# Moving GpSimd's drain from a critical section's exit to the end of its own gather stream

## The chip, the cores and the metric

One core of one Trainium2 chip. The metric is the device time of one execution in microseconds. Every time below is a median over repeated executions unless it is called a single run. "Span" is the length of the profiled execution, about 1.7 us shorter than the device time of the same execution.

## The reference

```python
B, S, N, D = (16, 4096, 2048, 512)
gathered = x[b_idx, indices, :].copy()      # x [B,S,D] f32, indices [B,N], sorted
cs = np.cumsum(gathered, axis=1)            # running sum along the gathered rows
return np.matmul(cs, w).astype(np.float32)  # w [D,D]
```

67 MB of rows are gathered and 67 MB of results stored.

## The kernel before

The kernel is written engine by engine, with its own semaphores, inside one critical section. GpSimd generates 256 gathers of 128 rows, ScalarE casts the gathered tiles and evicts results, TensorE does triangular sums and the projection, VectorE carries the running sum, and SyncE issues the stores. `pool.need(s, v)` makes GpSimd wait until semaphore `s` has reached `v`; `sp.need` does the same for SyncE. There are T = 256 gathers, R = 2 of them to a group, G = 128 groups, NG = 16 gather buffers and NO = 8 output buffers. The parts that matter here:

```python
ctx.enter_context(tc.tile_critical(no_gpsimd_drain=False))
# ... (cut)
def gather(t):
    g, r = divmod(t, R)
    pool.need(s_c, g + 1 - NG // R)          # a buffer is free again
    # ... (cut: which index column)
    nc.gpsimd.indirect_dma_start(
        out=g32[g % (NG // R)][:, r, :], out_offset=None, in_=x_flat,
        in_offset=bass.IndirectOffsetOnAxis(ap=ap, axis=0),
        element_offset=(t // NT) * S * D,
    ).then_inc(s_g[t % NG], 16)
# ... (cut) SyncE: all stores, then it waits until the last ones have landed
for g in range(G):
    store(g)
for g in range(G - NO, G):
    sp.need(s_o[g % NO], 16 * (g // NO + 1))
# ... (cut) GpSimd: two masks, then all gathers
for t in range(T):
    gather(t)
```

When the section ends, SyncE, which by then has waited for the last stores, raises a semaphore. Each of the five engines answers it with a drain, and SyncE waits for the five answers, for GpSimd's with its no-op. After that comes the program's closing barrier, in which GpSimd has three more drains of its own. None of this is in the source; it stands in the built program.

Of the kernel before, what the change touches and what calls it, by code (L numbers as in the profile page):

```python
# [27 lines left out]
def kernel(  # L28
# [7 lines left out]
    nc = tc.nc  # L36
# [38 lines left out]
    pa = [ps.tile([P, DC, R, Q], FP32, name=f"pa{i}") for i in range(NA)]  # L75
    pb = [ps.tile([P, R, D], FP32, name=f"pb{i}") for i in range(NB)]

    ctx.enter_context(tc.tile_critical(no_gpsimd_drain=False))  # L78

    def sem(name):  # L80
        return tc.alloc_semaphore(name)
# [17 lines left out]
    def gather(t):  # L99
        g, r = divmod(t, R)  # L100
        pool.need(s_c, g + 1 - NG // R)
        if t < FIRST:
            pool.need(s_first, 16)
            ap = idx_first[:, t, 0:1]
        else:
            pool.need(s_prep, t // P + 1)
            ap = idxg[:, t // P, t % P : t % P + 1]
        nc.gpsimd.indirect_dma_start(  # L108
            out=g32[g % (NG // R)][:, r, :],
            out_offset=None,  # L110
            in_=x_flat,
# [3 lines that stand above are left out]
# [103 lines left out]
    ).then_inc(s_ut, 1)  # L218
    for t in range(T):
        gather(t)  # L220


    for k in range(KI):
# [65 lines left out]
```

## Time and profile before

| | before |
|---|---|
| device time | 357.12 us median of 3 (356.56 to 357.59) |
| span of the profiled run | 354.6 us |
| bytes moved | 135.92 MB, about 415 GB/s in the body |
| GpSimd's drain at the exit | 348.56 to 353.53 us |

The instructions that matter are not counted as busy work: drains, no-ops and semaphore instructions stand in the views with a "q" behind the engine's name (POOLq is GpSimd's sequencer) and only when a source line is asked for. So the busy rows of the page show an empty end, and the queue's waits and the lines of the exit tell what fills it.

### The profile page before, as it was taken

How to read it: one execution, taken by the hardware profiler on the slowest of the kernel's cores; microseconds unless marked ns; L12 is line 12 of the kernel's file. 1: busy time of each engine (PE TensorE's matmuls, PEld its weight loads, DVE VectorE, ACT ScalarE, POOL GpSimd, SP SyncE). 2: the span in 40 equal slices, each digit the busy share in tenths (PEclk: the TensorE clock that was granted, in tenths of full speed). 3: DMA queues.
4: the chain of work that ended last, by engine and by line, in shares of the span. 5: the costliest groups of instructions: out<-in, count | busy, mean ns of one | idle time of the engine just before them, and what ended most of it. 6: DMA issues, size and time to landing. Idle time of an engine off the chain costs nothing.

```text
span 354.6 us, 5833 instructions
## 1 busy us (share of the span) xinstructions
PE 301.8 (85%) x2050; PEld 149.2 (42%) x2050; DVE 178.1 (50%) x260; ACT 257.9 (73%) x258; POOL 243.7 (69%) x264
## 2 busy tenths in 40 slices
PE   0497799999899999899898988989989889898880
PEld 0253354444354444444444444444444444444440
DVE  1354465555555555555554554645555555555530
ACT  0776687787788787777777777877878778687760
POOL 6777777777777777777777777777777777774000
PEclk9999999999999999999999999999999999999995
DMA  6789999999999999999999999999999999999761
GB/s 222 224 241 384 409 410 401 415 411 418 412 417 416 415 414 415 413 416 416 415 415 414 414 413 413 411 417 415 413 417 413 416 413 414 412 415 414 293 244 74
DMA packets 40029, 135.92 MB, mean 383 GB/s; under 512 B 6465, under 2 KB 6721, under 8 KB 40001
## 3 DMA queue, kind: packets, MB, share of 16 engines
q0 software_dynamic: 20480, 67.13, 48.5%
q1 hardware_dynamic: 19520, 68.43, 47.8%
q8 instruction: 17, 0.28, 0.3%
q14 instruction: 12, 0.09, 0.1%
HBM read 68.42 MB, written 67.11 MB: 382 GB/s over the span
## 4 chain that ended last, share of the span: by engine, by line
POOL 50%; DMA 22%; issue 17%; PE 5%; ACT 3%; ACTq 0%; SPq 0%
POOL g L108 50%; DMA g<-in_x_dram,idxg 21%; PE pb L160 4%; ACT g L120 3%; PE pa L128 1%; ACT ob L172 1%; DMA idx_first<-in_indices_dram 1%; ACTq L23 0%; SPq L284 0%; SPq L78 0%
## 5 line engine op out<-in xcount | busy, mean ns | idle before, releaser
L108 POOL DMA_INDIRECT g<-in_x_dram,idxg x254 | 240.5, 947 | 77.4 <-issue 71.3
L160 PE MATMUL pb<-w,cst 128*128 128x512 f16 x1024 | 263.5, 381 | 0.0
L148 DVE TENSOR_TENSOR cst<-pa,cst 128x512 f16<-128x512 f32 x240 | 166.0, 692 | 138.1 <-PE pa L128 137.3
L120 ACT CAST g<-g 128x1024 f16<-128x1024 f32 x128 | 133.6, 1045 | 66.9 <-issue 32.2
L172 ACT COPY ob<-pb 128x1024 f32<-128x1024 f32 x128 | 129.2, 1010 | 11.4 <-PE pb L160 9.8
L128 PE MATMUL pa<-ut,g 128*128 128x128 f16 x1024 | 101.1, 222 | 38.5 <-ACT g L120 37.8
L128 PEld LDWEIGHTS pa<-ut,g 128*128 128x128 f16 x1024 | 69.4, 99 | 128.4 <-ACT g L120 97.6
L160 PEld LDWEIGHTS pb<-w,cst 128*128 128x128 f16 x1024 | 90.0, 98 | 62.0 <-issue 1.1
L143 DVE CAST cst<-pa 128x512 f16<-128x512 f32 x16 | 11.1, 692 | 20.4 <-PE pa L128 20.4
L120 ACT ACT_TABLE_LOAD x1 | 1.3, 1283 | 9.5 <-DMA g<-in_x_dram,idx_first 9.5
L229 PE MATMUL pb<-ident,idxf 128*128 128x128 f32 x2 | 0.9, 462 | 4.2 <-DVE idxf L225 4.2
L108 POOL DMA_INDIRECT g<-in_x_dram,idx_first x2 | 2.1, 1043 | 1.6 <-DMA idx_first<-in_indices_dram 1.3
L225 DVE CAST idxf<-idx 128x128 f32<-128x128 uint32 x2 | 0.5, 226 | 4.1 <-DMA idx<-in_indices_dram 4.1
L229 PEld LDWEIGHTS pb<-ident,idxf 128*128 128x128 f32 x2 | 0.4, 182 | 4.4 <-issue 4.2
L252 ACT CAST w<-w 128x2048 f16<-128x2048 f32 x1 | 1.9, 1892 | 0.0
L234 DVE CAST idxg<-pb 128x128 uint32<-128x128 f32 x2 | 0.6, 292 | 0.3
L198 POOL MEMSET ident<- 128x128 f32 x1 | 0.2, 205 | 0.5 <-SPq L78 0.5
L201 POOL TENSOR_SCALAR_AFFINE_SELECT ident<-ident 128x128 f32<-128x128 f32 x1 | 0.3, 288 | 0.1
L273 POOL MEMSET const-float32-0.0<- 128x1 f32 x1 | 0.1, 100 | 0.3 <-issue 0.3
L210 POOL TENSOR_SCALAR_AFFINE_SELECT ut<-ut 128x128 f16<-128x128 f16 x1 | 0.3, 292 | 0.0
L199 POOL MEMSET ut<- 128x128 f16 x1 | 0.2, 206 | 0.0
L273 POOL MEMSET const-uint8-127<- 128x1 uint8 x1 | 0.1, 117 | 0.0
(2 smaller groups left out, 0.2 us busy)
## 6 DMA issues: line engine op xcount, KB each, us to landing
out_dram<-ob SPq DMA_DIRECT2D x128, 512.0 KB, 7.2
g<-in_x_dram,idxg POOLq DMA_INDIRECT x254, 10.2
w<-in_w_dram SPq DMA_DIRECT2D x1, 1024.0 KB, 5.6
idx<-in_indices_dram SPq DMA_DIRECT2D x2, 128.0 KB, 2.3
g<-in_x_dram,idx_first POOLq DMA_INDIRECT x2, 5.1
idx_first<-in_indices_dram SPq DMA_DIRECT2D x1, 2.0 KB, 1.9
```

The source lines that it names most:

```text
L108: nc.gpsimd.indirect_dma_start(out=g32[g % (NG // R)][:, r, :], out_offset=None, in_=x_flat, in_offset=bass.IndirectOffsetOnAxis(ap=ap, ax ...
L120: nc.scalar.copy(out=g16[g % NH][:], in_=g32[g % (NG // R)][:]).then_inc(s_c, 1)
L128: mm = nc.tensor.matmul(out=pa[t % NA][:, c], lhsT=g16[g % NH][:, r, c * P : (c + 1) * P], rhs=ut[:], start=(c == 0), stop=(c == DC - 1),)
L143: nc.vector.tensor_copy(out=dst, in_=pa[t % NA][:]).then_inc(s_d, 1)
L148: nc.vector.tensor_tensor(out=dst, in0=pa[t % NA][:], in1=last.unsqueeze(2).broadcast_to([P, DC, R, Q]), op=mybir.AluOpType.add,).then_inc ...
L160: mm = nc.tensor.matmul(out=pb[g % NB][:, j], lhsT=cst[g % NC][:, c, j, :], rhs=w16[:, c, :], start=(c == 0), stop=(c == DC - 1),)
L172: nc.scalar.copy(out=ob[g % NO][:], in_=pb[g % NB][:]).then_inc(s_e, 1)
L201: nc.gpsimd.affine_select(out=ident[:], in_=ident[:], compare_op=mybir.AluOpType.is_equal, fill=0.0, base=0, pattern=[[-1, P]], channel_mu ...
L225: nc.vector.tensor_copy(out=idxf[:, k, :], in_=idx64[:, k, 0::2]).then_inc(s_if, 1)
L229: nc.tensor.transpose(out=pb[k % NB][:, 0, :P], in_=idxf[:, k, :], identity=ident[:]).then_inc(s_pt, 1)
L234: nc.vector.tensor_copy(out=idxg[:, k, :], in_=pb[k % NB][:, 0, :P]).then_inc(s_prep, 1)
L252: nc.scalar.copy(out=w16[:], in_=w32[:]).then_inc(s_wc, 1)
```

## The change

The intent is to take GpSimd's drain off the end of the program: it drains in its own stream, behind its last gather, where it has nothing else to do, and the exit asks GpSimd for a no-op only.

```diff
-    ctx.enter_context(tc.tile_critical(no_gpsimd_drain=False))
+    ctx.enter_context(tc.tile_critical(no_gpsimd_drain=True))
 ...
     for t in range(T):
         gather(t)
+    nc.gpsimd.drain()
```

The closing barrier and its drains are the same in both.

## The prediction

> **What bounds the kernel now.** I read the page's slices first, because the change touches no arithmetic and I wanted to know where the span stops being limited by the steady state.
>
> ```profile
> POOL 6777777777777777777777777777777777774000
> ...
> DMA  6789999999999999999999999999999999999761
> GB/s 222 224 241 384 409 410 401 415 411 418 412 417 416 415 414 415 413 416 416 415 415 414 414 413 413 411 417 415 413 417 413 416 413 414 412 415 414 293 244 74
> ```
>
> From the fourth slice to the 37th the DMA engines are at nine tenths or more and move about 415 GB/s: the body is bound by bytes, 67 MB gathered and 67 MB stored. One slice is 354.6/40 = 8.87 us. In the last slice the traffic falls to 74 GB/s, so a slice at the end is nearly empty. GpSimd, which issues the gathers, is done about three slices before the end. The diff touches only GpSimd's stream after its last gather and the exit, so next comes the timeline of the end (start, duration, then engine and work; releaser in brackets).
>
> ```profile
> 322.66 0.95 POOL L108 DMA_INDIRECT g<-in_x_dram,idxg  x1 [0.30 <-issue]
> ...
> 344.63 1.01 ACT L172 COPY ob<-pb 128x1024 f32<-128x1024 f32 x1 [0.71 <-PE pb L160]
> 345.67 0.33 SPq L178 DMA_DIRECT2D out_dram<-ob  x1
> ```
>
> GpSimd's last gather is generated at 322.66 + 0.95 = 323.6 us. The last eviction ends at 345.64, the last store is issued at 345.67. After that no engine computes, yet the span ends at 354.6, which is 8.9 us later. Three stretches of that end (columns: length, busy time of PE, weight loads, DVE, ACT, GpSimd, granted clock, DMA share, GB/s):
>
> ```profile
> 345.60:348.50 2.90, 0.00 (x0) 0.00 (x0) 0.00 (x0) 0.04 (x1) 0.00 (x0) 0.71 0.60 242
> 348.50:353.60 5.10, 0.00 (x0) 0.00 (x0) 0.00 (x0) 0.00 (x0) 0.00 (x0) 0.50 0.00 0
> 353.60:354.60 1.00, 0.00 (x0) 0.00 (x0) 0.00 (x0) 0.00 (x0) 0.00 (x0) 0.50 0.00 0
> ```
>
> The first stretch is the last stores landing. In the second, 5.1 us long, nothing computes and nothing moves. What SyncE's queue waits for from 345 us on, and the instructions of the section's exit (line 78: count, duration in ns min/median/max, first and last start), say why:
>
> ```profile
> SPq L78 <- POOLq L78: 4.8, 1, 4.8
> SPq L23 <- DMA out_dram<-ob: 2.1, 2, 1.5
> ...
> L78 SPq NOP  x2: 13/16/18, 0.8 to 353.6; - x2
> ...
> L78 ACTq DRAIN  x1: 8/8/8, 348.6 to 348.6; - x1
> L78 POOLq DRAIN  x1: 4965/4965/4965, 348.6 to 348.6; - x1
> L78 DVEq DRAIN  x1: 17/17/17, 348.6 to 348.6; - x1
> ```
>
> At 348.6, once SyncE has seen the last stores land, every engine drains. Four of them take 7 to 17 ns; GpSimd takes 4965 ns, and SyncE's no-op at 353.6 waits for it: 4.8 us of wait, 1.3% of the time. The page's chain of work that ended last stops at ACT's copy at 344.63; the drain, not counted as busy, does not show in it. Behind the exit comes the program's own closing barrier (line 284), which also has drains on GpSimd:
>
> ```profile
> L284 POOLq DRAIN  x3: 34/34/123, 353.6 to 354.3; - x3
> ```
>
> These cost 34, 123 and 34 ns, directly behind the long one.
>
> **What the Trainium skill says.** "Perfetto Trace Analysis", section "Sequencer-only Instruction (DRAIN, etc)", says that for such an instruction the profiler's start is the moment all its semaphores are satisfied. So the 4965 ns are the drain itself and not its wait for SyncE; the trace agrees, as it starts at 348.6 together with the others'. "PSUM — Partial Sum Buffer", on sequencer-only instructions and completion, says that "drain waits for the engine to go fully idle", while a no-op is no sign of completion. "DMA: Bandwidth & Descriptors", section "SWDGE vs HWDGE vs iDMA", says that GpSimd's DMAs are descriptors that its own cores compute in software and append to rings in SBUF. Only GpSimd has such software here, and only its drain is long; that fits a drain which settles those rings, but no row shows what the drain does. VectorE's page, "VectorE: DVE Perf Modes", section "The DRAIN you can't avoid", gives runtime drains as about 12 ns on all five engines; the 4965 ns here disagree for GpSimd, and the measurement decides.
>
> **The change part by part.** 1. It adds one drain to GpSimd's stream, directly behind the 256th gather, at 323.6. 2. At the exit it replaces GpSimd's drain by a no-op which waits for the same semaphore from SyncE and answers on the same one; the other four engines' drains stay. The built instruction streams of PE, DVE, ACT and SyncE are otherwise equal. 3. The closing barrier keeps GpSimd's three drains, the first of which now follows the no-op.
>
> Part 1 costs nothing on the path if it is over by 348.5. Two sizes: the drain just takes 4965 ns, over at 328.6; or it also waits for the gathers in flight. The packets of GpSimd's queue end at 337.0, and then another 4965 ns gives 342.0. Both are ahead of 348.5, with 19.9 and 6.5 us to spare. GpSimd has nothing else to do then, and all gathers are already issued, so no transfer starts later.
>
> Part 2: before, the path is: SyncE's signal 348.52, drain 348.56 to 353.53, SyncE's no-op 353.55. After: signal 348.52, GpSimd's no-op at 348.56 for about 0.02 (SyncE's own is 13 to 18 ns). SyncE is then itself still collecting the other engines' answers: its last such instruction starts at 348.743 and takes 28 ns, so its no-op can run at about 348.80. The saving is 353.55 - 348.80 = 4.75 us, which agrees with the 4.8 of the wait view.
>
> Part 3: if the first closing drain stays at 34 ns, it adds nothing. Sum: 357.12 - 4.75 = 352.4 us, ratio 1.0135.
>
> **The rivals.** (a) The drain is deferred, not removed: the first drain after GpSimd has been standing idle for 25 us pays, whichever it is. Then the closing drain takes the 4.97 us and the time stays at 357.1. For it: all the cheap closing drains follow an expensive one immediately, so the trace never shows a late first drain cheap. Against it: the very first drain of the program takes 187 ns, part of that under a memset, with no gather yet issued; the long one is the only one with gathers between it and the one before. No packet moves between 348.5 and 353.6, so it isn't an instruction fetch that the trace would show. (b) The early drain settles only what has landed by 323.6. A gather takes 10.2 us at the median to land and 1.25 us to issue, so some 8 to 12 of 256 are then in flight. If the cost is per gather, 4965/256 = 19 ns each, the closing drain would pay about 0.2 us: 352.6. If it is a fixed cost for rings with anything in them, it would pay all of 4.97 again: 357.1. (c) The early drain disturbs the last transfers, by work on the rings while 10 gathers are in flight. The last casts wait for such gathers (the cast at 335.47), so a delay there would reach the end; a loss of up to 1 us is my guess at its size, 353.4. Nothing in the profile speaks for it.
>
> **Range and chances.** I give 0.77 to the full saving, landing at 351.6 to 353.0, since the three runs of before spread over 1.0 us; 0.08 to a part of it (rival b per gather, or c), 353 to 355.5; 0.15 to none of it, 356.5 to 357.7. A range of 351.4 to 355.5 then holds it somewhat over 8 times in 10. Faster by over 2% needs 350.0 or less, that is 7.1 us saved: more than the whole drain, and the rest of the tail is stores landing and the barrier, which stay. Slower by over 2% would need 7 us of new wait. So: faster 0.01, within 2% 0.98, slower 0.01.
>
> **What would show it right or wrong.** Right: a GpSimd drain starting at about 323.6, over before 348.5; no 5 us stretch without traffic after the last store; SyncE's wait for GpSimd at the exit under 0.2 us; closing drains still at tens of ns; a span of about 349.8. The early drain's length (5 or up to 18 us) tells whether it waits for the gathers in flight. Wrong: a closing drain on GpSimd of about 4.9 us, with the span still at 354.6 (rival a, or b with a fixed cost), or casts late at the end with landing times over the present ones (c).

## The result, and the profile after

| | before | after |
|---|---|---|
| device time, median of 6 | 356.99 us (356.45 to 357.88) | 352.50 us (351.85 to 353.14) |
| span of the profiled run | 354.6 us | 351.3 us |
| GpSimd at the exit | drain, 4965 ns | no-op, 13 ns |
| SyncE's exit signal to its no-op | 5.03 us | 0.29 us |

The ratio is 0.9872, 95% interval 0.9851 to 0.9893. A ratio here is the mean time of one kernel's fast runs over that of the other's in the same rounds, so not quite the ratio of the medians.

The slices of the profiled run after, to be held against those of before: GpSimd's row, DMA share and GB/s in 40 slices of 8.8 us.

```profile
POOL 6777777777777777777777777777777777776000
DMA  6789999999999999999999999999999999999854
GB/s 219 229 233 378 408 411 412 416 414 417 416 417 414 417 415 415 415 414 416 413 417 413 416 411 407 414 414 417 412 417 411 417 413 416 411 414 416 345 229 181
```

The body is the same, near 415 GB/s. Only the end is shorter: the last slice now averages 181 GB/s instead of 74. Three stretches of the end (length; busy time of PE, weight loads, DVE, ACT, GpSimd; granted clock; DMA share; GB/s):

```profile
345.80:350.00 4.20, 0.00 (x0) 0.00 (x0) 0.00 (x0) 0.00 (x0) 0.00 (x0) 0.80 0.42 170
350.00:350.40 0.40, 0.00 (x0) 0.00 (x0) 0.00 (x0) 0.00 (x0) 0.00 (x0) 0.50 0.00 0
350.40:351.30 0.90, 0.00 (x0) 0.00 (x0) 0.00 (x0) 0.00 (x0) 0.00 (x0) 0.50 0.00 0
```

The dead stretch of 5.1 us between the last store and the closing barrier has shrunk to 0.4. GpSimd's instructions by source line, after (count; duration in ns min/median/max; first and last start): the exit (78), the new drain (221) and the closing barrier (285).

```profile
L78 POOLq NOP  x1: 13/13/13, 350.0 to 350.0; - x1
...
L221 POOLq DRAIN  x1: 21874/21874/21874, 318.3 to 318.3; - x1
...
L285 POOLq DRAIN  x3: 34/41/123, 350.1 to 351.1; - x3
```

The new drain runs from 318.3 to 340.2, some 10 us ahead of the exit, and the closing drains stay at tens of ns.

One trap lies in comparing just these two profiles. Their spans differ by 3.3 us, not by 4.7. In the run after, SyncE, having seen its last store land, signals the exit at 349.99 instead of 348.52, 1.47 us later. Most of this, 1.3 us, is that this store took 3.6 us from its issue to its last packet where it took 2.3 in the run before. Adding the 1.47 back gives 3.27 + 1.47 = 4.74 us, which is the difference of the two exits, 5.03 - 0.29. The same store took 2.3 us in the profiles of experiments 1, 2 and 3 and 3.6 in that of experiment 4, so a profiled pair carries 1.3 us of chance here. Why it varies stayed open.

### The profile page after: what moved, and what is told of

Read it like the earlier page. It is cut to its first block, busy times and chain, and to the rows that moved or that the text cites. A ratio compares the mean times of both kernels' runs of the same rounds, so it can differ in the third digit from the quotient of the medians.

```text
span 351.3 us, 5834 instructions
## 1 busy us (share of the span) xinstructions
PE 301.2 (86%) x2050; PEld 149.0 (42%) x2050; DVE 178.2 (51%) x260; ACT 258.1 (73%) x258; POOL 243.7 (69%) x264
## 4 chain that ended last, share of the span: by engine, by line
POOL 48%; DMA 26%; issue 17%; PE 4%; ACT 3%; POOLq 0%; ACTq 0%; SPq 0%
POOL g L108 48%; DMA g<-in_x_dram,idxg 25%; PE pb L160 3%; ACT g L120 2%; PE pa L128 1%; DMA idx_first<-in_indices_dram 1%; POOLq L221 0%; ACT ob L172 0%; ACTq L23 0%; SPq L285 0%; SPq L78 0%
```

## The experiments

Three theories could explain the result. A: gathers leave work behind for GpSimd (a debt, below), and whichever drain comes first after them does it, once. B: GpSimd's first drain after a long idle time is long. C: the drain is long because of where it stands, at the exit.

The runs of experiments 1 to 4 are from one chip and share the runs of before (356.85 us, median of 11).

### 1. Both drains

```diff
-    ctx.enter_context(tc.tile_critical(no_gpsimd_drain=True))
+    ctx.enter_context(tc.tile_critical(no_gpsimd_drain=False))
```
(against the changed kernel)

> Both drains: the early one and the exit's own. Theory A (the long time is work that gathers leave behind, and whichever drain comes first after them settles it once): early drain 318 to 340 us as in the changed kernel, exit drain 0.03 to 0.2 us, time 352.3 to 352.7, ratio to before 0.987. Theory B (an idle GpSimd pays at its next drain): exit drain, some 8 to 10 us after the early one, still several us; time 355 to 357. Theory C (the exit's drain is long by its place or form): exit drain 4.97 us, time 357.

352.11 us (6 runs), ratio 0.9868, interval 0.9841 to 0.9896. The exit's own drain, after the early one, is back in its place:

```profile
L78 POOLq DRAIN  x1: 41/41/41, 348.3 to 348.3; - x1
```

It takes 41 ns instead of 4965. C falls, and the exit's flag is worth nothing beside the early drain: the saving comes from the early drain alone.

### 2. The exit's flag alone

```diff
-    ctx.enter_context(tc.tile_critical(no_gpsimd_drain=False))
+    ctx.enter_context(tc.tile_critical(no_gpsimd_drain=True))
```
(against the kernel before, with no drain behind the gathers)

> The exit leaves GpSimd out, and there is no early drain. Theories A and B: the first closing drain of the program now takes 4.9 to 5.0 us instead of 0.034, time 356.8 to 357.1, ratio 0.999 to 1.000: this half alone gains nothing. Theory C (place or form of the exit's drain): closing drains stay under 0.2 us, time 352.5, and the early drain would be idle decoration.

356.94 us, ratio 1.0013, interval 0.9979 to 1.0047: no gain. GpSimd's drains in the closing barrier, and the line of SyncE's waits from 345 us on (us in total, times, longest):

```profile
L284 POOLq DRAIN  x3: 40/123/4965, 349.1 to 354.7; - x3
```

```profile
SPq L284 <- PEq L284: 5.5, 2, 4.8
```

The 4965 ns have moved to the next drain in GpSimd's stream, to the nanosecond. The wait view puts SyncE's wait down to TensorE, the engine whose signal of the closing barrier it saw last; the cause is GpSimd's drain, which holds the barrier for all. A wait for a barrier with many members has to be read with the durations beside it.

### 3. Drain after the gathers have landed

```diff
+    for t in range(T - NG, T):
+        pool.need(s_g[t % NG], 16 * (t // NG + 1))
     nc.gpsimd.drain()
```

> The changed kernel, but GpSimd first waits for the semaphores of its last 16 gathers, and drains then. It tells what part of the 21.9 us of the early drain is waiting. Theory A with settling work only after landing: drain starts at 337.0 to 337.6, takes 4.9 to 5.0 us, ends at about 342.3. If part of the work is done while gathers are still in flight: it ends at about 340.2 as before and takes about 3 us. If it only waits for landing: under 0.2 us. The time is 352.3 to 352.8 in all three, since even 342.5 lies 6 us ahead of the exit.

352.49 us (4 runs), ratio 0.9881, interval 0.9845 to 0.9917.

```profile
L223 POOLq DRAIN  x1: 4965/4965/4965, 338.1 to 338.1; - x1
```

Once the gathers have landed, the drain takes the same 4965 ns as at the exit. So the 21.9 us of the changed kernel's drain come apart. Its record starts at 318.30, while four gathers were still queued ahead of it; generation ends at 323.46 (5.2 us). The last packet of GpSimd's queue ends at 337.20 (13.7 us). The drain ends 2.98 us later. As 2.98 is less than 4.97, part of the work is done while the gathers are still in flight.

### 4. A drain too late to hide

```diff
+    pool.need(s_e, G)
     nc.gpsimd.drain()
```

The drain now waits for the last eviction.

> The changed kernel, but the drain waits for the last eviction (345.7 us) before it starts. Theory A: it takes 4.97 us, ends at 350.7, and SyncE waits for it from its own 348.8 to 350.3: 0.4 to 1.9 us of the saving are given back, depending on how fast the last stores land; time 353.0 to 354.2, ratio 0.990 to 0.992. A rival by which the drain is cheap once the gathers have long landed (8 us): drain under 0.5 us, time 352.5.

354.09 us (6 runs), ratio 0.9911, interval 0.9881 to 0.9940: 1.6 us of the 4.5 are given back, by the medians. The late drain, the exit's no-op and SyncE's wait:

```profile
L222 POOLq DRAIN  x1: 4965/4965/4965, 346.4 to 346.4; - x1
```

```profile
L78 POOLq NOP  x1: 13/13/13, 351.5 to 351.5; - x1
```

```profile
SPq L78 <- POOLq L78: 0.5, 1, 0.5
```

The drain ends at 351.4, and only what sticks out behind the last store counts. In the profiled run that is 0.5 us, since its last store took 3.6 us to land; with a store of 2.3 us it would be 1.3 us more. What decides is whether the drain ends before the stores have landed.

### 5 to 8. How the cost grows (durations only)

These four single runs fell on another chip, on which the kernel before took 415.9 us and the body ran at 300 to 350 GB/s. Their times (442.8, 450.2, 439.5 and 443.6 us) say nothing about the change and none of the times expected can be checked; the drains' durations can.

Experiment 5 puts a drain ahead of the last gather, and 6 puts one half way, both in the kernel before (so with the exit's drain):

```diff
     for t in range(T):
         gather(t)
+        if t == T - 1 - 1:        # experiment 6: T - 128 - 1
+            nc.gpsimd.drain()
```

> The kernel before with one more drain, ahead of the very last gather; the exit's drain stays. One gather lies between it and the exit. If the drain's cost is a fixed sum due after any gather: exit drain 4.97 us. If it is per gather (4965 ns / 256 = 19 ns): exit drain 0.04 to 0.06 us. The last gather is held back until the others have landed and been settled, at about 340 us by the changed kernel's early drain, and lands some 3 us later, so its group's chain ends some 4 to 6 us later than now: time 361 to 363 in the first case, 356 to 358 in the second.

> As the run before, with the drain half way, 128 gathers ahead of the exit. Fixed: exit drain 4.97 us. Per gather: 128 x 19 ns = 2.5 us. The drain half way waits for the gathers in flight (10 us) and 3 us more, while no new ones start: GpSimd's row shows a hole of 13 to 16 us, and 2 to 6 us of it reach the end, so 359 to 363 if fixed, 2.5 us less if per gather.

Experiment 7 has both drains and writes the last 8 stores twice more:

```diff
+    for again in (2, 3):
+        for g in range(G - NO, G):
+            store(g)
+        for g in range(G - NO, G):
+            sp.need(s_o[g % NO], 16 * (g // NO + again))
```
(against experiment 1)

> Early drain and exit drain as in the run with both, and the last 8 stores are written two times more, so that the end comes some 15 to 25 us later and GpSimd stands idle for 25 to 35 us between its two drains (same result, longer time on purpose: 368 to 378 us). Theory A: exit drain 0.03 to 0.2 us. Theory B (idling for 20 us or more makes the next drain long): 4.97 us.

Experiment 8 has both drains, with one plain transfer between them:

```diff
     nc.gpsimd.drain()
+    nc.gpsimd.dma_start(out=spare[:], in_=w[0:P, :]).then_inc(s_x, 16)
+    pool.need(s_x, 16)
```
(against experiment 1; the lines that make the tile and the semaphore are cut)

> As the run with both drains, with one plain transfer (128 rows of w into a spare tile) issued by GpSimd after the early drain and waited for, then the exit's drain. If any software-issued transfer leaves the cost behind: exit drain 4.97 us, time 357. If only the indirect gathers do: 0.04 us, time 352.5.

The exit's drain in experiment 5, 6, 7 and 8, one line each (in 8 the section stands one line lower):

```profile
L78 POOLq DRAIN  x1: 136/136/136, 439.8 to 439.8; - x1
```

```profile
L78 POOLq DRAIN  x1: 2504/2504/2504, 444.9 to 444.9; - x1
```

```profile
L78 POOLq DRAIN  x1: 41/41/41, 436.5 to 436.5; - x1
```

```profile
L79 POOLq DRAIN  x1: 136/136/136, 440.6 to 440.6; - x1
```

Experiment 7 settles B: after 44 us of idling between its two drains the second takes 41 ns. B falls, A stands. Experiments 5 and 6 say that the cost is no fixed sum. The line through 128 and 256 gathers has a slope of 19.2 ns, but one gather costs 136 - 41 = 95 ns, five times as much, so something in the picture "19 ns per gather" was wrong. A plain transfer costs the same 136 ns as a gather, which neither expectation for experiment 8 had allowed for: it is not only the gathers, and it is not the whole sum.

### 9 to 12. The missing points, and the price of a drain in mid-stream

On a normal chip again (before: 357.26 us, median of 7). 9 repeats 6 for its time; 10 and 11 put the drain 32 and 8 gathers ahead of the exit; 12 has both drains with 32 plain transfers of 16 bytes each between them.

```diff
     nc.gpsimd.drain()
+    for i in range(32):
+        nc.gpsimd.dma_start(out=spare[0:1, 4*i : 4*i+4], in_=w[0:1, 4*i : 4*i+4]).then_inc(s_x, 16)
+    pool.need(s_x, 16 * 32)
```
(experiment 12 against experiment 1; the tile, the semaphore and a `with` line around the loop are cut)

> The drain half way once more, now for its time (the chip of the earlier run moved its data slower, so its times say nothing). Exit drain 2.50 us again, 2.46 us less than before. The drain half way leaves a hole of 12 to 15 us in GpSimd's row; the gathers' queue stands empty for some 4 to 5 us of it, and since the body is bound by bytes, 2.5 to 5 us of that are lost: time 357 to 360, so the half of the cost that is taken off the exit is paid again in the body. If the prefetched tiles hide the hole wholly: 354.5.

> The drain 32 gathers ahead of the exit. Per gather: exit drain 0.04 + 32 x 0.0192 = 0.66 us; a fixed sum would be 4.97. Same hole as half way, so 355 to 358; 352.8 if the hole is hidden.

> The drain 8 gathers ahead of the exit. Straight line through 128 and 256 gathers: exit drain 0.04 + 8 x 0.0192 = 0.20 us. One gather gave 0.136, which lies over that line (0.06); if there is a small fixed part once any gather has run, this gives 0.27 or so.

> As the run with both drains, with 32 plain transfers of 16 bytes issued by GpSimd between the early drain and the exit's. If the cost is per transfer: exit drain 0.66 us, as for 32 gathers of 128 rows. If it is per packet or per row: clearly less, down to 0.14 us. The time is later by the issue of the 32 transfers, 20 to 40 us, on purpose.

The exit's drain in 9, 10, 11 and 12:

```profile
L78 POOLq DRAIN  x1: 2504/2504/2504, 356.5 to 356.5; - x1
```

```profile
L78 POOLq DRAIN  x1: 2667/2667/2667, 357.1 to 357.1; - x1
```

```profile
L78 POOLq DRAIN  x1: 707/707/707, 355.8 to 355.8; - x1
```

```profile
L79 POOLq DRAIN  x1: 2667/2667/2667, 358.1 to 358.1; - x1
```

My expectations for 8 and 32 gathers (0.2 and 0.66 us, or 4.97) were both wrong. All points together, each read from profiled executions:

| transfers since the last drain, all landed | the next drain, ns |
|---|---|
| 0 | 41 |
| 1 (gather, or plain) | 136 |
| 8 gathers | 707 |
| 32 gathers | 2667 |
| 32 plain of 16 bytes | 2667 |
| 128 gathers (twice) | 2504 |
| 256 gathers (before, and experiments 2, 3, 4) | 4965 |

From 1 to 8 the slope is (707 - 136)/7 = 81.6 ns, from 8 to 32 it is (2667 - 707)/24 = 81.7. So up to 32 transfers the drain pays 82 ns for each that GpSimd has issued since its last drain, whether large or small: 32 transfers of 16 bytes cost what 32 gathers of 128 rows cost, although they add 1024 packets to GpSimd's queue where those gathers have 2560. Then the line breaks: 128 gathers cost less than 32. With 54 + 82 n ns, the 2504 stand for 30 transfers and the 4965 for 60. That fits a stream in which most of the debt is paid on the way, in steps of 98 (or 49), and only the rest is left for the drain: 128 - 98 = 30, 256 - 2 x 98 = 60. A side check agrees. A drain started while gathers are in flight ends, on the normal chips, 1.76 us after the last packet with 128 gathers before it (experiment 9), 1.67 with 224 (10), 2.65 with 248 (11) and 2.98 with 256; that is 0.5 us plus half the debt of 30, 28, 52 and 60 transfers. But no run has a count between 32 and 128, so where and by whom the steps are taken is a fit and not shown, and so is why half the debt can be paid while waiting. The trace of the kernel before speaks against a pause of GpSimd: 98 times 82 ns is 8 us, but no gather took over 1.14 us there and none starts more than 1.45 us after the one before it. If the debt is paid on the way, it is in parts too small to show as a pause of GpSimd.

The times: 9 took 361.36 us, ratio 1.0125 (1.0081 to 1.0169), and 10 took 362.06, ratio 1.0138 (1.0098 to 1.0177); the single runs of 11 and 12 took 359.29 and 363.87. The times expected were missed: 357 to 360 for 9, 355 to 358 for 10, and 20 to 40 us of delay for 12, which came 11.8 us after experiment 1 (for 11 none was named). In 9 the exit's drain is 2.46 us shorter and the whole is 4.1 us longer, so the drain half way costs about 6.6 us, more than the 2.5 to 5 that I expected. In 10 the same sum gives 4.8 + 2.3 = 7.1 us. The profile of experiment 9 around that drain, in GpSimd's timeline and as two stretches (columns as above), with the same stretches of the kernel before below:

```profile
162.15 0.95 POOL L108 DMA_INDIRECT g<-in_x_dram,idxg  x1 [0.30 <-issue]
174.66 0.94 POOL L108 DMA_INDIRECT g<-in_x_dram,idxg  x1 [11.57 <-ACT g L120]
```

```profile
172.00:178.00 6.00, 3.75 (x26) 1.71 (x24) 2.31 (x4) 1.96 (x2) 2.73 (x3) 1.00 0.67 242
178.00:190.00 12.00, 8.10 (x48) 4.17 (x48) 4.15 (x6) 6.32 (x7) 8.95 (x11) 0.86 0.87 274
```

```profile
172.00:178.00 6.00, 5.26 (x39) 2.65 (x38) 3.00 (x6) 4.06 (x6) 4.48 (x6) 1.00 1.03 416
178.00:190.00 12.00, 10.85 (x74) 5.21 (x73) 6.37 (x10) 9.57 (x10) 8.95 (x11) 1.00 1.03 415
```

The releaser named for the hole of 11.57 us, ScalarE's cast, is only the last semaphore of that wait; the drain from 153.5 to 173.9 is what held GpSimd. Traffic falls to 242 and 274 GB/s after it: (416 - 242) x 6 + (415 - 274) x 12 = 2.7 MB not moved, which at 415 GB/s is 6.6 us. That this equals the cost is chance of where the stretches end: from 190 to 200 and from 200 to 220 us the traffic is still at 364 and 398 GB/s, where the kernel before has 417 and 413, which makes 0.8 MB or 2.0 us more. Some 2 us of the sum are made up at the end, where the kernel before runs out of gathers first (from 330 to 340 us 256 GB/s, here 410); the last eviction ends 6.8 us later than before, at 352.48. So in a body bound by bytes most of the hole is paid, and its tail, in which the pipeline fills again, is more than half of it; I had counted the empty queue alone.

No run beat the changed kernel clearly: the version with both drains, which leaves the exit as it was, is the same within the intervals (0.9868 against 0.9872).

## Why the prediction was right

The prediction of 352.4 us, range 351.4 to 355.5, met a measured 352.50. Its ratio of 1.0135 is before over after; turned round it is 0.9867, against 0.9872 measured. That it came within 0.1 us is partly luck, as single runs of the changed kernel lie up to 1.3 us apart.

- Part 2, the saving. 4.75 us were predicted from one exit's records; the two exits differ by 4.74. By the medians it is 4.49 us, by the ratio 4.57; the ratio's interval allows 3.8 to 5.3 us. The span of 349.8 that it named was missed in the profile (351.3), by the 1.47 us of the late exit signal.
- Part 1, the early drain is hidden: right, it ended at 340.2, between the two sizes named (328.6 and 342.0) and nearer the later. It waits for the gathers in flight, as the second size had it, but from the last packet on it took 2.98 us and not 4.97. Its start was given as 323.6; the record starts at 318.3, since it counts the time in which the drain waits for its own engine.
- Part 3, the closing drains stay cheap: right, 41, 123 and 34 ns.
- Rival (a), an idle engine pays: excluded by experiment 7.
- Rival (b): the drain did settle everything, since it waits for the gathers in flight. The 19 ns per gather on which its smaller branch rested is wrong: the runs show 82 ns per transfer for up to 32, and a debt after 256 gathers as large as that of 60 at this price. It didn't touch the sum, as nothing was left for the closing drain.
- Rival (c), disturbed transfers: not seen. The last gather's packets end at 337.2 (before: 337.0), and its cast starts 0.2 us later in the profiled pair. That is within what runs differ by: the packets end at 336.8 in experiment 1, which has the early drain, and at 337.5 in experiment 2, which has none.
- What the prediction missed: the flag in the diff does nothing by itself. Alone it moves the cost to the closing barrier (experiment 2); without it the early drain brings the same (experiment 1).

## What to carry to other kernels

Look at the end of the span for a stretch in which nothing computes and nothing moves, and then at the durations of the drains of the lines that end the program; busy rows and the chain of work may hide 5 us there. Where GpSimd issues transfers and ends early, one drain behind its last transfer takes the debt off the end; it must be over before the last stores land, and it must not stand in mid-stream, where here it cost 6.6 us. Check a change of two lines by its halves: here one half did all the work, and the exit could have kept its drain.

## What the Trainium skill lacked or had wrong

- "VectorE: DVE Perf Modes", section "The DRAIN you can't avoid", tells two things called DRAIN apart, the flush after a VectorE operation and the runtime's own of about 12 ns on all five engines. It lacks a third, the drains that the program itself has at a section's exit and in its closing barrier (lines 78 and 284 here). On ACT, TensorE, VectorE and SyncE these took 7 to 17 ns, on GpSimd 34 to 4965 ns, so the 12 ns must not be carried over to them.
- No page has what GpSimd's drain costs after software-issued transfers; it would belong to "DMA: Bandwidth & Descriptors", section "SWDGE vs HWDGE vs iDMA". The runs show 41 ns with none, 136 with one, 707 with 8, 2667 with 32 (of 16 bytes or of 128 rows alike), 2504 with 128 and 4965 with 256, payable at the first drain after them wherever it stands.
- The same section says nothing of a drain and transfers in flight. Here the drain also waits for their landing: it ended 2.98 us after the last packet of its queue, and 4.97 us after its start where all had landed.
- "Perfetto Trace Analysis", section "Sequencer-only Instruction (DRAIN, etc)", starts the record when the semaphores are satisfied. That agrees (the exit's drain starts at 348.56, after SyncE's signal at 348.52), but the section lacks that a drain's record then includes the wait for the engine's own queue: 5.2 of the 21.9 us here.
